# Row factors by a matmul, squares behind splits, a load table for the second phase's weights, and tiles placed elsewhere, in a hybrid decoder layer

## The chip, the cores and the metric

The kernel runs on one core of a Trainium2 chip. Its engines work side by side, each through its own queue in order: TensorE (PE) for matmuls, VectorE (DVE), ScalarE (ACT), GpSimd (POOL), and SyncE (SP), which issues most of the transfers. The metric is the device time of one execution in microseconds (us); shown is the median of three runs. A profile is one further execution taken with the hardware profiler.

## The reference

One decoder layer over 4096 new prompt tokens and 64 sample tokens (8 sequences of 8), width 1024:

```python
h = _rmsnorm(x, g_pre)
z = h @ w_in                          # (tokens, 1024) @ (1024, 2816)
cb, cc, ch, cg, q, k, v, ag, mq, mg = _split_cols(z)
conv = conv_w[0] * up[:, 0:t] + conv_w[1] * up[:, 1:t + 1] + conv_w[2] * up[:, 2:t + 2]   # up: cc * ch
out_a = jax.nn.silu(cg) * cb * conv
out_b = jax.nn.silu(ag) * o_b         # sliding-window attention of q, k, v with sinks
out_c = jax.nn.silu(mg) * o_c         # cross-attention of mq into 256 memory tokens
y = jnp.concatenate([out_a, out_b, out_c], axis=-1) @ w_out
return x + _rmsnorm(y, g_post), new_conv, new_k, new_v

def _rmsnorm(x, g):
    r = lax.rsqrt(jnp.mean(xf * xf, axis=-1, keepdims=True) + RMS_EPS)
    return (xf * r).astype(x.dtype) * g
```

The change lies in the product `h @ w_in`. Its row factors are the `r` of `_rmsnorm`: one number for each token.

## The kernel before

**The product.** The 4160 tokens are 8 blocks of 520 (`NBLK`), each two halves of 260. Tokens lie along the free dimension, channels on the 128 partitions. The 22 column tiles of `w_in` are done in three phases (`PHASES`, line 43): phase 0 takes four pairs of tiles (gates, q/k, v), phase 1 four pairs (the conv columns), phase 2 three pairs (the rest of q and mq). A pair and its index `q` is called a quad member; `q` runs over the pairs of a phase. A block of x and a pair of weights are each cut into 2 x 2 quarters, and Winograd's form of Strassen's method makes the product of them in seven steps instead of eight; `PRODUCTS` (line 40) has for each step `p` the weight operand and the x operand:

```python
PRODUCTS = (("A11", "B11"), ("A12", "B21"), ("S2", "T2"), ("S3", "T3"), ("S1", "T1"), ("S4", "B22"), ("A22", "T4"))
```

A step is written (phase, block, p). Weights that begin with S and x operands that begin with T are sums of quarters. Every operand is split in two parts that the matmul takes at full rate, hi (an ACT copy to the rounded type) and lo (a DVE subtraction); a product of one quad member is 4 x 3 matmuls (`product`, line 278: hi*hi, hi*lo, lo*hi), so a step of phases 0 and 1 is 48 matmuls of 260 columns and a step of phase 2 is 36. `w_split` (line 139) splits weights, `split` (270) and `x_split` (488) x. `evict` (286) adds the accumulators (PSUM, tags x and y in turn, two of each) into z tiles: by an ACT copy for p = 0 (line 292), by DVE otherwise (290).

**Blocks 0 and 1 of phase 0** are not done by the seven steps but by the plain eight (`PLAIN`, line 484, `plain_block`, 574), since the weights' S sums aren't there yet; here a step is written (block, s). While PE works on them, the S weights are summed (`first_sums`, 504) and split (`first_fills`), and the gate and q/k/v results are finished (`done`). What is issued beside each of the 16 plain steps stands in the table of `plain_jobs` (532); a step's jobs are dealt out behind its four products. x isn't scaled by its row factors ahead of these products: `z_rows` (525) scales z instead. From block 2 on x is scaled first (`x_gain` on ACT by the norm weight, `x_scale` on DVE by the row factors).

**The row factors.** `row_load` (203) brings 104 tokens' rows (a "nat" tile, two buffers); `row_step` (213) squares them on ACT with a running sum, five steps a block. After the fifth, POOL takes mean and power -0.5 and scatters the 520 numbers to DRAM (line 228); two row queues later SP reads them back into all 128 partitions (`rows_load`, 199: tile rb). Square j frees the buffer that load j + 2 waits for.

**Order.** In phase 0 and up to the change to phase 1, `manual_schedule` keeps each engine's instructions, DMA issues too, in the order of the program. Behind that (`in_order.close()`, line 709) a scheduler orders them by its own estimate. `flush` (119) issues the stores that were put off, at the start of the next step: by POOL's queue in phase 0, by SP's from phase 1 on (`store_queue`).

**Changes of phase.** `open_phase` (92) closes the phase's tile pools and opens those of the next in the same memory: temps (`tp`, 7, 9 and 4 buffers of 2088 bytes a partition), in phase 0 the row tiles (`natp`), and z tiles (`zp`, 5, 7 and 3). A tile of a new pool waits until what lay in its bytes is done with. Before, temps are opened first, so phase 1 has its temps over phase 0's temps, and phase 2 its z tiles over phase 1's temps. The next phase's weights are loaded in block 7: at step p + 1 those that step p used, into temps (`w_load`, 143), and split one step later (lines 728 to 739). So A11 is loaded at (0,7,1), and so on to S4, loaded at (0,7,6) and split ahead of (1,0,0), and A22 in (1,0,0).

## Time and profile before

| | us |
|---|---|
| median of three runs (lowest, highest) | 1684.39 (1681.62, 1684.4) |
| the profiled execution's own time | 1686.34 |
| its span, from first to last instruction | 1684.6 |
| granted TensorE clock, mean | 0.975 |
| DMA traffic | 306.15 MB, 182 GB/s over the span |

By stretch of the span, from counts of the matmuls of line 283: plain blocks 0 and 1 from 8.7 to 125.8 us, the rest of phase 0 to 377.5, phase 1 to 715.0, phase 2 to about 982, and attention with the output projection to the end.

The profile is read as follows. The page's first lines give each engine's busy time and share of the span; then follow 40 equal slices of the span with a digit for the busy tenths, and the clock that TensorE was granted in tenths. A timeline row has start, length, engine, line, operation, out<-in, count, and in brackets the idle time of the engine before it with what ended it. SPq and POOLq are the queues from which transfers are issued; the length there is that of the issue, not of the transfer. A row of the waits has the total, the number and the longest. A row of the chain of waits has start, length and what. In a row of windows the numbers behind the engine's busy time are counts of instructions.

### The profile page before, as it was taken

The numbers are of one execution on the slowest core, as the hardware profiler recorded it, in microseconds if no ns is written. First come the engines' busy times: TensorE is split into PE (matmuls) and PEld (weight loads), VectorE is DVE, ScalarE is ACT, GpSimd is POOL, SyncE is SP. The second block draws the span as 40 slices with busy tenths as digits, with TensorE's granted clock in tenths as the row PEclk, the third lists the DMA queues.
The fourth block names the chain that finished last, engine by engine and source line by source line (L and its number), as shares of the span: only waits on it lengthen the run. The fifth ranks groups of instructions, "written<-read, shape, count | busy, mean of one in ns | idle before, by whom it ended". The sixth has DMA issues, their size and how long they took to land.

```text
span 1684.6 us, 29573 instructions
## 1 busy us (share of the span) xinstructions
PE 1585.2 (94%) x11073; PEld 1401.4 (83%) x11073; DVE 1182.1 (70%) x2113; ACT 791.2 (47%) x2028; POOL 349.7 (21%) x590
## 2 busy tenths in 40 slices
PE   7969999998999999989999966999999999999998
PEld 7969999998999999988999953677777777777766
DVE  5548878897888778965666665766777766767743
ACT  6566556574322222533434345655555555555522
POOL 0113222211000000000000024444433344343320
PEclk9979999999999999999999977999999999999999
DMA  7778999877555333669766587767677766666152
GB/s 227 159 184 226 265 254 256 246 262 256 188 186 173 115 115 128 214 196 276 262 204 246 186 225 152 145 139 146 143 155 155 164 136 135 147 147 133 51 184 88
DMA packets 175412, 306.15 MB, mean 182 GB/s; under 512 B 31142, under 2 KB 104614, under 8 KB 175238
## 3 DMA queue, kind: packets, MB, share of 16 engines
q1 hardware_dynamic: 129061, 228.34, 43.6%
q0 software_dynamic: 46208, 75.93, 23.3%
q8 instruction: 88, 1.44, 0.3%
q14 instruction: 55, 0.44, 0.1%
HBM read 197.07 MB, written 108.12 MB: 181 GB/s over the span
## 4 chain that ended last, share of the span: by engine, by line
PE 43%; DVE 17%; ACT 7%; issue 3%; DMA 3%; POOL 3%; ACTq 0%; SPq 0%; POOLq 0%; DVEq 0%
PE c L283 30%; PE y L1213 6%; ACT sm L954 5%; DVE sm L960 3%; DVE sm L944 2%; DVE wmx L946 2%; DMA wor<-in_w_out 2%; POOL xp L909 2%; PE wt L964 1%; DVE yn L1220 1%; PE xs L901 1%; PE wo L827 1%; DVE xr L1231 1%; DVE mix L928 1%; ACT xp L905 1%
## 5 line engine op out<-in xcount | busy, mean ns | idle before, releaser
L1213 PE MATMUL y<-wo,mh 128*128 128x512 f32 (+1 forms) x1072 | 350.8, 391 | 1.4 <-DVE mh L1190 1.4
L290 DVE TENSOR_TENSOR z<-c,z 128x520 f32<-128x520 f32 (+1 forms) x308 | 194.9, 647 | 91.3 <-PE c L283 86.0
L1213 PEld LDWEIGHTS y<-wo,mh 128*128 128x128 f32 x1072 | 200.4, 188 | 42.0 <-issue 2.8
L1213 PE MATMUL y<-wo,ml 128*128 128x512 f32 (+1 forms) x520 | 202.2, 389 | 0.0
L954 ACT ACTIVATE sm<-sm,wnm 128x128 f32<-128x128 f32 x256 | 99.9, 391 | 75.7 <-DVE wnm L948 75.6
L1213 PEld LDWEIGHTS y<-wo,ml 128*128 128x128 f32 x520 | 98.1, 189 | 15.2
L941 PE MATMUL ws<-kst,q 128*128 128x256 f32 x512 | 81.8, 302 | 8.8 <-ACT sm L943 5.9
L971 POOL TENSOR_SCALAR_AFFINE_SELECT wpv<-wpt 128x512 f32<-128x512 f32 x62 | 40.0, 645 | 224.8 <-ACT wpt L966 223.9
L941 PEld LDWEIGHTS ws<-kst,q 128*128 128x128 f32 x512 | 68.3, 197 | 11.3 <-ACT sm L943 6.4
L902 DVE TENSOR_REDUCE xmx<-xs 128x2 f32<-128x512 f32 x64 | 44.2, 691 | 43.6 <-PE xs L901 43.6
L905 ACT ACTIVATE xp<-xs,xnm 128x256 f32<-128x256 f32 x128 | 59.4, 469 | 27.3 <-DVE xnm L903 27.0
L943 ACT COPY sm<-ws 128x256 f32<-128x256 f32 x128 | 44.5, 371 | 56.9 <-PE ws L941 54.0
L909 POOL TENSOR_SCALAR xp<-xp,xrd 128x256 f32<-128x256 f32 x128 | 62.9, 498 | 37.9 <-DVE xrd L906 35.1
L1221 ACT ACTIVATE y<-y 128x512 f32<-128x512 f32 (+1 forms) x66 | 38.8, 588 | 66.6 <-DVE yn L1220 66.6
L843 POOL MEMSET kst<- 128x512 f32 x1 | 0.5, 525 | 324.9 <-DVE cacc L389 324.9
L1220 DVE TENSOR_TENSOR yn<-y,gpost 128x512 f32<-128x512 f32 (+1 forms) x66 | 45.2, 684 | 30.4 <-PE y L1213 30.3
L222 ACT ACTIVATE nat<-nat 104x1024 f32<-104x1024 f32 x40 | 42.3, 1058 | 48.2 <-DMA nat<-in_x_p 48.0
L1231 DVE SCALAR_TENSOR_TENSOR xr<-yn,yst,xr 128x1024 f32<-128x1024 f32 (+2 forms) x34 | 42.5, 1253 | 29.9 <-POOL yst L1227 29.9
L964 PEld LDWEIGHTS wt<-ident,sm 128*128 128x128 f32 x256 | 28.0, 144 | 40.3 <-issue 18.1
L901 PE MATMUL xs<-mk,q 128*128 128x256 f32 x256 | 47.9, 311 | 12.3 <-ACT xp L905 8.5
L960 DVE TENSOR_TENSOR sm<-sm,wrd 128x512 f32<-128x512 f32 x64 | 54.9, 858 | 2.0
L914 PEld LDWEIGHTS xt<-ident,xp 128*128 128x128 f32 x256 | 29.7, 143 | 31.2 <-PE wo L827 12.2
(935 smaller groups left out, 5119.8 us busy)
## 6 DMA issues: line engine op xcount, KB each, us to landing
q<-qd POOLq DMA_DIRECT2D x64, 384.0 KB, 6.0
mix<-md SPq DMA_DIRECT2D x16, 1024.0 KB
xr<-in_x_p SPq DMA_DIRECT2D x32, 512.0 KB
nat<-in_x_p SPq DMA_DIRECT2D x39, 416.0 KB
o_yp<-xr SPq DMA_DIRECT2D x31, 512.0 KB
md<-th POOLq DMA_DIRECT2D x48, 260.0 KB, 7.0
qd<-zh SPq DMA_DIRECT2D x48, 260.0 KB
qd<-z SPq DMA_DIRECT2D x48, 260.0 KB
```

The lines of the kernel that those rows point to most:

```text
L283: TE.matmul(bank[:, :HW], l, r, start=first and i == 0, stop=last and i == 3 * KH - 1)
L290: add = lambda dst, other: V.tensor_tensor(dst, c, other, op=ALU.add)
L901: TE.matmul(s[:, i, :], q[:, i * P : i * P + P], third["mk"][:, part, h, :], start=part == 0, stop=part == 1)
L905: S.activation(p[:, i, :], s[:, i, :], AF.Exp, bias=nm[:, i : i + 1], scale=SCALE, accum_out=den[:, i : i + 1])
L909: G.tensor_scalar(p[:, i, :], p[:, i, :], rd[:, i : i + 1], 0.5, op0=ALU.mult, op1=ALU.mult)
L941: TE.matmul(s3[:, hh, :], self.q[:, 4 + 2 * (2 * half + hh) + kvh, i * P : i * P + P], self.kst[:, 2 * kvh + part, i * P : i * P + 2 * P], ...
L954: S.activation(sm[:, hh, :], sm[:, hh, :], AF.Exp, bias=nm[:, hh : hh + 1], scale=SCALE, accum_out=den[:, hh : hh + 1])
L960: V.tensor_tensor(sm, sm, rd.unsqueeze(2).to_broadcast([P, 4, P]), op=ALU.mult)
L964: TE.transpose(t[:, hh * P : (hh + 1) * P], sm[:, hh, :], ident)
L1213: TE.matmul(acc, self.hl[l][:, k], wo[k][:, r, c0:c1], start=j == 0, stop=j == passes * KT - 1)
L1220: V.tensor_tensor(yn[:m, c0:c1], acc[:m], gpost[:m, c0:c1], op=ALU.mult)
L1231: V.scalar_tensor_tensor(self.xr[:m, cs], yn[:m, cs], st[:m, 3:4], self.xr[:m, cs], op0=ALU.mult, op1=ALU.add)
```

## The change

Four things are changed.

1. *Block 2's row factors.* They aren't scattered to DRAM and read back. `rows_diag` makes on DVE a 104 x 520 tile of five diagonal blocks (identity times factors), `rows_product` multiplies it by a tile of ones on PE, which puts each token's factor into all 128 partitions, and ACT copies the result into the rb tile. All other blocks keep the way through DRAM.
2. *Squares behind splits.* In the table of `plain_jobs` from (0,5) on, squares (`*row`) are moved behind x splits, weight fills and finishing work; one of the twenty squares goes to step (0,2,0). The gates' copy of the sample tokens in block 0 goes from ACT to DVE.
3. *Weights at the change to phase 1* (code phase 1, the second) are loaded and split by a table, `SWITCH`, which goes ahead of a step's other jobs: A11 and S2 through the row tiles, A12 through temps, and S3, S1, S4 and A22 only in block 0 of phase 1. For the last phase the old rule stays.
4. *Places.* z tiles are opened ahead of temps in phases 1 and 2, and the row tiles ahead of temps in phase 0. So phase 1 has z over the row tiles, phase 0's temps and a little of its z, and temps over the rest of phase 0's z; phase 2 has z over phase 1's z.

```diff
+    ones = const.tile([P, P], F32, name="ones")
+    G.memset(ones, 1.0)
...
-        tp = own.enter_context(tc.tile_pool(name=f"t{ph}", bufs=(7, 9, 4)[ph]))
+
         if ph == 0:
             natp = own.enter_context(tc.tile_pool(name="nat", bufs=2))
+            tp = own.enter_context(tc.tile_pool(name="t0", bufs=7))
         zp = own.enter_context(tc.tile_pool(name=f"z{ph}", bufs=(5, 7, 3)[ph]))
+        if ph > 0:
+            tp = own.enter_context(tc.tile_pool(name=f"t{ph}", bufs=(9, 4)[ph - 1]))
...
+            if b == PLAIN_BLOCKS:
+                nat["first"] = r
+                return
             G.dma_start(rowd[b].rearrange("(i p) -> p i", p=RG), r[:RG, 0:5])
             row_spreads[b] = 2
+
+    def rows_diag():
+
+        t = nat["diag"] = temp("diag")[:RG, : 2 * HW]
+        for i in range(5):
+            V.tensor_scalar(t[:, RG * i : RG * (i + 1)], ident[:RG, :RG], nat["first"][:RG, i : i + 1], None, op0=ALU.mult)
+
+    def rows_product():
+
+        acc = pa2.tile([P, 2, 512], F32, tag="y", name="rows_y", bufs=2)[:, :, :HW]
+        for half in range(2):
+            TE.matmul(acc[:, half], ones[:RG], nat["diag"][:, HW * half : HW * half + HW], start=True, stop=True)
+        rows[PLAIN_BLOCKS] = natp.tile([P, 2 * HW], F32, tag="rb", name="rb_first")
+        S.copy(rows[PLAIN_BLOCKS].rearrange("p (a n) -> p a n", a=2), acc)
...
-            S.copy(zs[:, zsi, :], th[:, :NS])
+            V.tensor_copy(zs[:, zsi, :], th[:, :NS])
...
-            if 1 <= p < 6:
+            if 1 <= p < 6 or (b, p) == (PLAIN_BLOCKS, 0):
                 jobs.append(row_step)
...
-            (0, 5): lambda: [*sums(1, 0), *row, *sums(1, 1), *fills(1, "S2"), *row, *fills(1, "S3")],
-            (0, 6): lambda: [*parts(1, "B11"), *fills(1, "S1", "S4"), *row, *sums(3, 0)],
-            (0, 7): lambda: [*fills(3, "S2", "S3"), *row, *fills(3, "S1"), *row],
-            (1, 0): lambda: [*parts(1, "B21"), *row, *z_rows(0, 1), *row],
-            (1, 1): lambda: [*z_rows(0, 0), *done(0, 1), *row, *row],
-            (1, 2): lambda: [*row, *done(0, 0)],
-            (1, 3): lambda: [*parts(1, "B12"), *sums(2, 0), *row],
-            (1, 4): lambda: [*sums(2, 1), *fills(2, "S2"), *gains(2, "B11"), *row],
-            (1, 5): lambda: [*parts(1, "B22"), *fills(2, "S3", "S1", "S4"), *gains(2, "B21")],
-            (1, 6): lambda: [*row, *gains(2, "B12"), *scales(2, "B11", "B21"), *row],
-            (1, 7): lambda: [lambda: h_split(0), *gains(2, "B22"), *scales(2, "B12"), lambda: t_sum(0, 2, "T1"), *row,
-                             *scales(2, "B22"), *z_rows(1, 1)],
+            (0, 5): lambda: [*sums(1, 0), *sums(1, 1), *fills(1, "S2", "S3"), *row],
+            (0, 6): lambda: [*parts(1, "B11"), *fills(1, "S1", "S4"), *row, *sums(3, 0), *row],
+            (0, 7): lambda: [*fills(3, "S2", "S3", "S1"), *row],
+            (1, 0): lambda: [*parts(1, "B21"), *z_rows(0, 1), *row, *row],
+            (1, 1): lambda: [*z_rows(0, 0), *done(0, 1), *row],
+            (1, 2): lambda: [*parts(1, "B12"), *row, *done(0, 0), *row],
+            (1, 3): lambda: [*row, *sums(2, 0), *sums(2, 1), *fills(2, "S2")],
+            (1, 4): lambda: [*parts(1, "B22"), lambda: rows_diag(), *gains(2, "B11", "B21"), lambda: rows_product()],
+            (1, 5): lambda: [*row, *fills(2, "S3", "S1", "S4"), *scales(2, "B11")],
+            (1, 6): lambda: [*gains(2, "B12"), *scales(2, "B21", "B12"), *row, *row],
+            (1, 7): lambda: [lambda: h_split(0), *gains(2, "B22"), *scales(2, "B22"), lambda: t_sum(0, 2, "T1"), *row,
+                             *z_rows(1, 1)],
...
+    def next_load(nph, q, o, dst=None):
+        if dst is None:
+            raws[q, o] = w_load(nph, q, o)
+        else:
+            raws[q, o] = dst
+            DMA.dma_start(dst, w_raw(PHASES[nph][q], o) if o[0] == "A" else sd[PHASES[nph][q]][o])
...
+    last = NBLK - 1
+    SWITCH = {(0, last, 1): lambda: next_loads("A11", True),
+              (0, last, 2): lambda: next_loads("A12"),
+              (0, last, 3): lambda: next_fills("A11"),
+              (0, last, 4): lambda: [*next_fills("A12"), *next_loads("S2", True)],
+              (0, last, 6): lambda: next_fills("S2"),
+              (1, 0, 0): lambda: next_loads("S3"),
+              (1, 0, 1): lambda: [*next_loads("S1"), *next_fills("S3")],
+              (1, 0, 2): lambda: [*next_loads("S4"), *next_fills("S1")],
+              (1, 0, 3): lambda: next_loads("A22"),
+              (1, 0, 4): lambda: next_fills("S4"),
+              (1, 0, 5): lambda: next_fills("A22")}
...
-            if i > 0 and steps[i - 1][0] < 2 and steps[i - 1][1] == NBLK - 1:
+            if i > 0 and steps[i - 1][0] == 1 and steps[i - 1][1] == NBLK - 1:
...
+            if (ph, b, p) in SWITCH:
+                jobs = SWITCH[ph, b, p]() + jobs
```

`next_loads(o, True)` takes two row tiles of 1024 columns, each for two weights of 512; `next_fills(o)` splits the four.

29 lines of the change are left out of this document (19 added, 10 removed).

## Prediction

> **What bounds the kernel now.** I read the page first, for the engine that is busy nearly throughout and for the slices where it is not.
>
> ```profile
> PE 1585.2 (94%) x11073; PEld 1401.4 (83%) x11073; DVE 1182.1 (70%) x2113; ACT 791.2 (47%) x2028; POOL 349.7 (21%) x590
> ...
> PE   7969999998999999989999966999999999999998
> ...
> PEclk9979999999999999999999977999999999999999
> ```
>
> TensorE (PE) sets the time; what can be won is its idle stretches. The change touches three of them: one in slice 3 (84 to 126 us, digit 6, with its clock low) and two short ones, near 390 and 725 us, that the tenths hardly show. A step of the plain blocks and of phases 0 and 1 is 48 matmuls, one of phase 2 is 36, so the start of a step is found by counting matmuls of L283. Then I asked for windows cut at these starts. Columns: window, length, PE busy, PEld, (DVE, ACT, POOL where shown,) clock, DMA share, GB/s.
>
> ```profile
> 74.33:80.08 5.75, 5.75 (x50) 5.72 (x48) 1.00 0.60 65
> 80.08:99.94 19.86, 0.18 (x3) 0.00 (x1) 0.63 0.86 212
> 99.94:108.53 8.59, 8.59 (x48) 8.36 (x49) 0.67 0.80 137
> 108.53:114.25 5.72, 5.72 (x51) 5.72 (x49) 1.00 0.72 190
> ```
> ```profile
> 377.52:383.64 6.12, 6.02 (x50) 5.81 (x49) 6.12 (x11) 3.81 (x9) 1.74 (x4) 1.00 0.28 84
> 383.64:398.36 14.72, 7.99 (x51) 7.38 (x49) 10.44 (x13) 6.05 (x11) 4.41 (x9) 0.88 0.84 297
> 398.36:406.60 8.24, 7.71 (x48) 7.31 (x49) 5.47 (x7) 3.14 (x7) 0.84 (x2) 0.79 0.70 239
> 423.88:430.88 7.00, 6.11 (x50) 5.91 (x49) 7.00 (x8) 2.60 (x4) 0.00 (x0) 1.00 0.44 130
> 442.38:449.08 6.70, 6.03 (x51) 5.82 (x49) 6.70 (x8) 1.31 (x2) 0.00 (x0) 1.00 0.47 105
> ```
> ```profile
> 719.40:731.99 12.59, 4.76 (x38) 4.35 (x37) 5.78 (x8) 2.76 (x4) 2.92 (x5) 0.93 0.86 207
> 731.99:738.71 6.72, 6.72 (x36) 6.72 (x37) 2.95 (x6) 3.59 (x9) 0.00 (x0) 0.62 0.96 311
> 738.71:743.06 4.35, 4.35 (x39) 4.35 (x37) 2.94 (x5) 1.47 (x2) 0.00 (x0) 1.00 0.21 68
> ```
>
> A full step is 5.75 us, in phase 2 4.35. So there are three stalls. **A**, in block 1 between its fourth and fifth product: 19.86 of waiting and 8.59 - 5.75 = 2.84 in the step after it, at a clock of 0.67: 22.7. **B**, phase 0 to 1: 0.37 + 8.97 + 2.49 + 1.25 + 0.95 over 5.75 in five steps of blocks 0 and 1: 14.0. **C**, phase 1 to 2: 8.24 + 2.37: 10.6. Together 47.3 us. Next I looked at what PE waited for, and what that waited for.
>
> ```profile
> PE c L283 <- ACT hi_1B L493: 19.7, 1, 19.7
> PE c L283 <- ACT w_0A L140: 8.7, 1, 8.7
> ```
> ```profile
> PE c L283 <- ACT z L292: 6.1, 1, 6.1
> PE c L283 <- DVE lo_0B L274: 1.7, 1, 1.7
> ```
>
> **A** waits for ScalarE (ACT) to split B12 of block 1. ACT works in order, and squares of rows stand ahead of that split, each waiting for its rows from DRAM:
>
> ```profile
> 66.32 1.06 ACT L222 ACTIVATE nat<-nat 104x1024 f32<-104x1024 f32 x1 [5.45 <-DMA nat<-in_x_p]
> 71.75 1.07 ACT L222 ACTIVATE nat<-nat 104x1024 f32<-104x1024 f32 x1 [1.63 <-DMA nat<-in_x_p]
> 79.98 1.06 ACT L222 ACTIVATE nat<-nat 104x1024 f32<-104x1024 f32 x1 [0.97 <-DMA nat<-in_x_p]
> 91.55 1.06 ACT L222 ACTIVATE nat<-nat 104x1024 f32<-104x1024 f32 x1 [6.94 <-DMA nat<-in_x_p]
> 99.38 1.72 ACT L493 ACTIVATE hi_1B<-xl1B,gpre 128x260 fp32r<-128x260 f32 x4
> ```
> ```profile
> 67.84 1.20 POOL L227 TENSOR_TENSOR r<-r,mhalf 104x5 f32<-104x5 f32 x1
> 69.35 1.01 POOL L228 DMA_DIRECT2D rowd<-r  x1 [0.31 <-POOL r L227]
> 79.65 0.36 SPq L201 DMA_DIRECT2D rb<-rowd  x1
> 73.00:81.00 8.00, 7.26 (x61) 7.05 (x59) 3.22 (x5) 4.04 (x10) 2.23 (x4) 1.00 0.72 74
> 81.00:84.00 3.00, 0.00 (x0) 0.00 (x0) 0.00 (x0) 0.66 (x3) 0.00 (x0) 1.00 0.90 315
> ```
>
> Counting squares from 0, these are 9, 11, 12 and 14; 9 ends block 1's rows, 14 block 2's. After 9, POOL takes the power and scatters the 520 factors to DRAM (69.35). From 73 to 81 all queues together move 74 GB/s, then 315; SP stands at the broadcast load of these factors until 79.65. So the scatter, not the squares' arithmetic, makes the rows late.
>
> **B**: the S4 weights are loaded late and their split holds ACT, behind it the copy of PE's accumulators (L292). **C**: the same copy waits for a store, since its z tile lies where a conv temp lay.
>
> ```profile
> 380.89 0.32 SPq L147 DMA_DIRECT2D wr_0S<-sd0S  x1
> 386.01 8.10 DMA wr_3S<-sd6S
> 394.13 0.62 ACT L140 CAST w_3S<-wr_3S 128x512 fp32r<-128x512 f32 x1 [0.96 <-DMA wr_3S<-sd6S]
> ```
> ```profile
> 723.94 7.31 DMA md<-cacc
> 731.35 0.87 ACT L292 COPY z<-c 128x520 f32<-128x520 f32 x2 [4.36 <-DMA md<-cacc]
> ```
>
> **The change, part by part.** *A, squares behind splits.* Up to (0,4) nothing moves. One square less in (0,5) and (0,7) puts the load of square 8 behind block 0's broadcast, where 9's stands now: square 8 starts at 66.32, and the split of B21 behind it is where it is now. Squares 9 and 10 follow at about 69.0 and 71.75. The three copies into zs that wait for VectorE (DVE) leave ACT for DVE (three times 0.24 and their waits; DVE has room, 3.22 busy of 8 us), which hides in square 11's wait for its rows. That load is issued where 12's is now, but square 9, and so the scatter, comes 69.0 - 66.3 = 2.7 later: the slow stretch runs from 75.7 to 83.7, and 11 lands before it, near 76. Then, in the new order, comes the split of B12: 77.2, and PE wants it at 80.08. The 19.86 us are gone at this place. If 11 lands inside the slow stretch as 12 does now (79.98), 1 to 2 us stay.
>
> *A, the product with ones.* Something else is late next. The two matmuls that spread block 2's factors stand in PE's queue at the end of (1,4), and PE takes its work in order: from there it waits for square 14, the power, and the diagonal. Square 14 starts now 10.5 us after the slow stretch ends; SP has the same broadcast and the same bytes ahead of it. So 83.7 + 10.5 = 94.2; with the square and its read-out (1.15) 95.4; POOL's two operations (square's end 67.47 to 69.04) 97.0. The diagonal is five DVE instructions of 104 columns, which the trace does not show; nearest are
>
> ```profile
> L386 DVE TENSOR_SCALAR cacc<-ub,convw x16: 453/486/493, 435.8 to 718.6; 128x520 f32<-128x520 f32 x14, 128x456 f32<-128x456 f32 x2
> L386 DVE TENSOR_SCALAR cacc<-us,convw x2: 251/255/259, 436.2 to 439.8; 128x64 f32<-128x64 f32 x2
> 769.20 1.72 PE mem_acc L654 x4
> ```
>
> so 5 x 0.25 to 5 x 0.49; 104 is nearer 64, 1.3: 98.3. The matmuls are f32 like those of L654, four instructions of 512 columns in 1.72; four of 260 take 0.87: 99.2. Fifth product ends at 80.08 + 5.75 = 85.8, PE idles 12.4, and its next step is cold again, 8.59. It ends at 107.8, where now it ends at 114.25: **6.5 us won**. What this path must also pass on DVE: the sums of S weights for the third pair, which now wait for a temp until a store behind block 2's scatter lands:
>
> ```profile
> 107.28 0.69 DVE L512 TENSOR_TENSOR wa2S<-wa2A,wa2A 128x512 f32<-128x512 f32 x1 [4.46 <-DMA md<-th]
> ```
>
> Block 2's scatter is gone, so I put this temp at 90 (an estimate: its tanh follows square 12 at 80 to 82, and its store lands after the slow stretch ends at 83.7); then 0.69 and five more of 0.61 for the sums, 0.6 for S2's split and 1.7 for the low half of B22 end before 97, under square 14. Bounds of A: square 14 never late, 22.7 - 0.9 = +21.8; that temp still at 107.28, then 107.3 + 3.7 + 0.6 + 1.7 + 1.3 + 0.9 = 115.5 against 108.53: -7.0. I take the value worked out from the landing, as nothing is left of what delayed the store. Square 19 and block 3's broadcast come one step later against a PE that is 6.5 us earlier; no row prices that, it lies between 0 and one step, 5.75, and I take 0, since the factors are used two steps after the load. The memset of ones lies under PE's first wait, the 8.7 us for w_0A on ACT, and costs nothing; without that cover it would be one small POOL instruction.
>
> The Trainium skill, "TensorE: Matmul & The Clock Gate", Part 1, says that the clock falls to half after an idle window of about 3.4 us and returns after 3.4 us of work, so an estimate from that page is 1.7 us lost after each long wait. The trace agrees that the step after a wait is slow, but with 2.84 us (99.94:108.53); with 1.7 for the cold step that stays, A's gain would be 7.6 instead of 6.5.
>
> *B, loads by a table.* A11 and S2 now go through the row tiles, S3, S1, S4 and A22 (16 tiles) are loaded in phase 1 with its nine temps and split one to two steps before use. The wait of S4 for a phase-0 temp (380.89) and ACT's hold until 394.13 go. What is late next: DVE. Sixteen subtractions of 0.61 are 9.7 us in seven steps of 5.75 that hold the eviction, split and sum work already; S3 is wanted 17.25 us after phase 1 starts, and its load waits for block 7's z tiles, now under the temps. Bounds: 0 and 14.0. I leave three steps at the 1.25 that 423.88:430.88 pays with DVE full: 4 stay, **10.0 won**.
>
> *C, other places.* In phase 2 z lies over phase 1's z tiles, which DVE alone reads, last for the cacc whose store is issued at 723.94, so the copy can go then and the step at 725.9 (the 1.7 for lo_0B stays) is not held: 6.1 and the cold 2.37: **8.5 won**, bounds 0 and 10.6.
>
> **Sum.** 6.5 + 10.0 + 8.5 = 25.0. The profiled execution took 1686.3 (span 1684.6 and 1.7 around it), giving 1661.3; it is 1.9 above the median of 1684.4, so the runs should show 1659.4. All three lie on PE's own queue, and behind each PE is full for hundreds of us.
>
> **Rivals.** (1) *The whole of A goes*: square 14's load is early because the bytes ahead of it moved before the scatter. For it: block 2's B21 no longer stands behind the broadcast on SP; against: it is issued into the slow stretch. 21.8 + 18.5: 1644.1. (2) *A only turns over*: the temp is as late as now, -7.0 + 18.5: 1672.9. For it is the row at 107.28, against it that its scatter is gone. (3) *It doesn't do what it says at a phase change*: z of phase 1 now lies over phase 0's temps, and a store in flight (7.31 in the row) holds the copy there; B won 0: 1669.4. Against: POOL's stores of that block are issued early once ACT isn't held. (4) *Slower*: in phase 1 SP carries stores too, in order with the loads. If a store that waits for its producer stands ahead of S3, S1, S4 and A22, each comes a step late: 4 x 5.75 and as many cold steps, 4 x 2.84: 34.4 lost where 14.0 are lost now: -20.4 + 15.0: 1689.8. It decides when S3's last tile lands more than 17 us into phase 1; 8.10 for one load speaks against it, unless it is issued 9 us late.
>
> **Chances.** Forecast 0.50 (its own range 1651 to 1667), (1) 0.12, (2) 0.15, (3) 0.15, (4) 0.08. From 1645 to 1677 all but (4) and half of (1) are held, and a little of the rest. A run tells 0.2%, 3.4 us, from no change; only (4) ends above, and milder forms of it near the old time: faster 0.89, same 0.04, slower 0.07.
>
> **What would show it.** After: the step (1,4) starts near 80 to 82 with no wait for hi_1B; then one wait of 10 to 14 us ahead of a matmul on rows_y, released by DVE's diag; only one broadcast of rows fewer on SP; no wait on ACT z L292 near 380 and 700; the summed excess of phase 1's first two blocks at 3 to 6 us, with DVE as releaser. A is wrong if PE's wait before rows_y is under 5 or over 18 us; B if S3's load is issued later than 9 us into phase 1; C if a store still releases L292.

## The result, and the profile after

The changed kernel takes 1673.65 us in the median of seven runs (1670.3 to 1678.51), the kernel before 1684.4 beside it (seven runs, 1680.71 to 1685.72): a ratio of 0.9944, 95% interval 0.9925 to 0.9962. By the medians it is 10.75 us faster; 25.0 were forecast. Ratios, here and below, are estimated from all executions but two slow ones (6048.44 us in all_three, and 1964.64 us in the kernel before beside tsum_first) and not from the medians, whose quotient differs from them by up to 0.0009. The profiled execution took 1678.51, the slowest of the seven, with a span of 1676.8, 7.8 below the span before. So 3 of the 10.75 us stand in no trace here, and all that follows is the 7.8.

The page's first lines after the change:

```profile
PE 1585.2 (95%) x11077; PEld 1401.8 (84%) x11077; DVE 1184.1 (71%) x2124; ACT 791.1 (47%) x2023; POOL 352.5 (21%) x590
...
PE   7967999998999999999999956999999999999998
...
PEclk9989999999999999999999977999999999999999
```

PE's busy time is the same to the tenth. The 6 of slice 3 is still there, so the stall of block 1 has only become shorter; the 7 behind it, where the kernel before has a 9, is new. Steps were found as before, by counting matmuls (now line 305). Windows of the changed kernel, columns as in the prediction:

```profile
80.66:101.20 20.54, 7.41 (x54) 6.95 (x53) 11.43 (x25) 10.25 (x24) 4.09 (x7) 0.72 0.91 274
101.20:108.05 6.85, 6.85 (x51) 6.75 (x49) 4.06 (x5) 5.12 (x11) 0.47 (x1) 0.86 0.26 72
132.05:145.70 13.65, 6.30 (x49) 5.90 (x49) 6.14 (x9) 4.33 (x8) 6.04 (x11) 0.94 0.85 164
145.70:154.45 8.75, 8.06 (x48) 7.76 (x49) 7.93 (x10) 3.62 (x6) 0.00 (x0) 0.70 0.97 285
```
```profile
380.91:394.14 13.23, 6.17 (x51) 5.76 (x49) 9.76 (x13) 6.00 (x12) 3.24 (x6) 0.97 1.01 356
394.14:402.66 8.52, 8.52 (x48) 8.52 (x49) 5.95 (x9) 4.20 (x7) 0.00 (x0) 0.65 0.89 338
431.40:437.41 6.01, 5.92 (x50) 5.71 (x48) 6.01 (x16) 1.91 (x3) 0.00 (x0) 1.00 0.69 18
437.41:447.24 9.83, 7.95 (x49) 7.54 (x50) 8.76 (x11) 1.21 (x2) 0.00 (x0) 0.83 0.82 235
717.75:724.05 6.30, 4.61 (x38) 4.40 (x37) 5.17 (x7) 2.25 (x5) 0.00 (x0) 1.00 0.65 141
724.05:728.34 4.29, 4.29 (x38) 4.29 (x37) 2.37 (x3) 1.27 (x3) 0.00 (x0) 1.00 0.88 320
```

The first fence is (1,4), (1,5), and then (0,2,2) and (0,2,3), two steps of block 2 that were 7.64 and 7.01 before and are 13.65 and 8.75 now: a stall the prediction doesn't have. In the second fence (1,0,1) and (1,0,2) are nearly as long as before, (1,1,2) has become long, and (2,0,1) and (2,0,2) are short. The waits of PE, largest ones:

```profile
PE rows_y L249 <- DVE diag L243: 13.1, 1, 13.1
...
PE c L305 <- ACT hi_2T L295: 6.9, 2, 6.5
...
PE c L305 <- ACT z L314: 4.4, 1, 4.4
```

The account by stretch, each figure the difference of two step starts (after minus before): at (1,6) **-6.2** (108.05 against 114.25). Block 2 gives back 8.24, so that block 3 starts 2.0 *later* than before (171.71 against 169.67). Blocks 3 to 7 win 4.4, and phase 1 starts 2.4 earlier (375.16 against 377.52). Its first two blocks lose 0.7, block 0 of phase 2 wins **7.2**, and everything behind loses 1.0. Rounded, the sum is the -7.8.

How far one profile can be trusted is seen from the runs below, which share long stretches of code with the changed kernel. In the nine that equal it up to block 2, (1,6) starts between 106.25 and 112.04 us; in the six that equal it in blocks 0 and 1 of phase 1, these take 12.2 to 15.7 us more than full steps, and block 0 of phase 2 takes 32.4 to 33.8 (33.8 in the changed kernel, 41.0 before). The stretch behind that block takes 923.6 to 936.1 us over all versions. Of the kernel before there is one profile. So C's gain is clear; differences of three or four microseconds in the other stages are not shown by one pair of profiles.

**Block 2.** What holds hi_2T, in the timelines of POOL and of ACT:

```profile
132.52 0.99 POOL L236 DMA_DIRECT2D rowd<-r  x1 [0.30 <-POOL r L232]
133.52 1.65 POOL L132 DMA_DIRECT2D md<-th  x3
```
```profile
141.99 0.62 ACT L346 CAST zh<-z 128x520 fp32r<-128x520 f32 x1 [8.40 <-DMA md<-th]
...
144.58 1.06 ACT L295 CAST hi_2T<-xl2B 128x1040 fp32r<-128x1040 f32 x1 [0.92 <-DVE xl2B L288]
```

Block 3's scatter goes out at 132.52 and the store of a finished gate behind it at 133.52, but that store lands only at 141.96. Its temp is what the cast to zh waits for, and the split PE needs stands behind the cast on ACT. From 132 to 142 all queues moved 90 GB/s. In the kernel before, the scatter, the cast, the split and PE's first matmul on it:

```profile
129.23 1.00 POOL L228 DMA_DIRECT2D rowd<-r  x1 [0.30 <-POOL r L227]
...
141.39 0.63 ACT L324 CAST zh<-z 128x520 fp32r<-128x520 f32 x1 [2.08 <-DMA md<-th]
...
144.30 1.06 ACT L273 CAST hi_2T<-xl2B 128x1040 fp32r<-128x1040 f32 x1 [1.23 <-DVE xl2B L266]
...
145.41 0.39 PE L283 MATMUL c<-hi_2T,w_0S 128*128 128x260 f32 x1 [0.47 <-ACT hi_2T L273]
```

So the cast waited for a store behind the scatter there too, and ran within 0.6 us of its time here, although the scatter went out 3.3 us earlier. There PE came for the split near 144.9 and waited 0.47 us; here it comes near 139.2 and waits 6.45.

**Change to phase 1.** SP's issues and ACT:

```profile
382.87 0.34 SPq L152 DMA_DIRECT2D wr_0S<-sd0S  x1
...
385.83 1.65 SPq L152 DMA_DIRECT2D wr_3S<-sd6S  x1
```
```profile
389.11 0.62 ACT L145 CAST w_0S<-wr_0S 128x512 fp32r<-128x512 f32 x1 [2.82 <-DMA wr_0S<-sd0S]
...
392.98 0.62 ACT L145 CAST w_3S<-wr_3S 128x512 fp32r<-128x512 f32 x1 [1.02 <-DMA wr_3S<-sd6S]
393.50 1.08 ACT L314 COPY z<-c 128x520 f32<-128x520 f32 x2
```

The copy of PE's accumulators stands behind S3's splits, and these wait for loads issued 7.7 us into phase 1. So one late load (S3's) has taken the place of another (S4's). **Change to phase 2**, where no store holds the copy any more:

```profile
722.31 0.87 ACT L314 COPY z<-c 128x520 f32<-128x520 f32 x2 [3.30 <-DVE cacc L411]
```

### The profile page after: what moved, and what is told of

Read it like the earlier page. It is cut to its first block, busy times and chain, and to the rows that moved or that the text cites. A ratio compares the mean times of both kernels' runs of the same rounds, so it can differ in the third digit from the quotient of the medians.

```text
span 1676.8 us, 29593 instructions
## 1 busy us (share of the span) xinstructions
PE 1585.2 (95%) x11077; PEld 1401.8 (84%) x11077; DVE 1184.1 (71%) x2124; ACT 791.1 (47%) x2023; POOL 352.5 (21%) x590
## 3 DMA queue, kind: packets, MB, share of 16 engines
q1 hardware_dynamic: 128917, 228.08, 44.2%
## 4 chain that ended last, share of the span: by engine, by line
PE 55%; DVE 18%; DMA 9%; ACT 8%; issue 5%; POOL 4%; SPq 0%; ACTq 0%; POOLq 0%; DVEq 0%
PE c L305 42%; PE y L1270 6%; ACT sm L1011 5%; DMA nat<-in_x_p 3%; DVE sm L1017 3%; DVE sm L1001 2%; DMA wor<-in_w_out 2%; DVE wmx L1003 2%; POOL xp L966 2%; DVE yn L1277 1%; PE wt L1021 1%; DMA rowd<-r 1%; PE xs L958 1%; DMA md<-th 1%; DVE mix L985 1%
## 5 line engine op out<-in xcount | busy, mean ns | idle before, releaser
L1270 PEld LDWEIGHTS y<-wo,ml 128*128 128x128 f32 x520 | 98.5, 190 | 15.4
L959 DVE TENSOR_REDUCE xmx<-xs 128x2 f32<-128x512 f32 x64 | 44.2, 691 | 43.4 <-PE xs L958 43.4
L1021 PE MATMUL wt<-ident,sm 128*128 128x128 f32 x256 | 42.8, 292 | 14.0 <-DVE sm L1017 8.1
```

The lines of the kernel that those rows point to most:

```text
L1021: TE.transpose(t[:, hh * P : (hh + 1) * P], sm[:, hh, :], ident)
L1270: TE.matmul(acc, self.hl[l][:, k], wo[k][:, r, c0:c1], start=j == 0, stop=j == passes * KT - 1)
```

## The experiments

The kernels ran in groups, each on one chip with runs of the kernel before beside them, and the chips differ (that kernel's medians were 1684.05, 1682.37, 1693.6, 1682.73, 1689.75 and 1688.48). So the ratio to the kernel before on the same chip is compared: the changed kernel's is 0.9944. Where an expectation names a time, it was reckoned from 1684.4 and 1673.65, so on another chip its ratio counts. Stages are read from the profiles. "Excess" is the time of fourteen steps, blocks 0 and 1 of phase 1, over 14 x 5.75: 14.06 before, 14.73 after.

| run | median, us | before, us | ratio | 95% interval |
|---|---|---|---|---|
| rows3 | 1672.31 | 1684.05 | 0.9929 | 0.9909 to 0.9948 |
| sq19 | 1670.87 | 1684.05 | 0.9920 | 0.9901 to 0.9938 |
| place1 | 1684.67 | 1684.05 | 1.0009 | 0.9995 to 1.0023 |
| table_old | 1683.30 | 1684.05 | 0.9990 | 0.9978 to 1.0002 |
| rows1 | 1671.24 | 1682.37 | 0.9931 | 0.9907 to 0.9955 |
| dram2 | 1679.72 | 1682.37 | 0.9985 | 0.9969 to 1.0001 |
| act_order | 1680.72 | 1682.37 | 0.9981 | 0.9965 to 0.9998 |
| pool_sub | 1677.60 | 1682.37 | 0.9967 | 0.9950 to 0.9984 |
| rows3b | 1677.01 | 1693.60 | 0.9906 | 0.9887 to 0.9924 |
| places2 | 1685.24 | 1693.60 | 0.9954 | 0.9939 to 0.9968 |
| rows13 | 1669.86 | 1693.60 | **0.9862** | 0.9845 to 0.9879 |
| best1 | 1670.03 | 1693.60 | 0.9866 | 0.9848 to 0.9885 |
| less_dve | 1673.25 | 1682.73 | 0.9948 | 0.9927 to 0.9969 |
| less_dve_places2 | 1675.32 | 1682.73 | 0.9947 | 0.9928 to 0.9965 |
| tsum_first | 1683.10 | 1689.75 | 0.9966 | 0.9952 to 0.9980 |
| tsum_first_places2 | 1682.97 | 1689.75 | 0.9964 | 0.9948 to 0.9980 |
| best2 | 1669.43 | 1689.75 | 0.9876 | 0.9854 to 0.9898 |
| all_three | 1680.75 | 1688.48 | 0.9949 | 0.9930 to 0.9969 |

### A: who takes the gain back in block 2

**rows3**, block 3's factors by the product as well:

```diff
-            if b == PLAIN_BLOCKS:
+            if b in (PLAIN_BLOCKS, PLAIN_BLOCKS + 1):
...
+        if ph == 0 and b == PLAIN_BLOCKS and p == 2:
+            jobs += [rows_diag, lambda: rows_product(b + 1)]
```

> Block 3's row factors too go by the product with ones (diagonal and product in step (0,2,2)), so that no scatter of 4-byte writes falls into block 2; all else as in the changed kernel. Theory (the gain of A is given back because block 3's scatter, issued at 132.5 us, makes POOL's stores behind it land at 142 to 146 and so holds the temp of the zh cast): steps (0,2,2) and (0,2,3), 13.65 and 8.76 us now, come to under 14 us together, the 6.45 us wait for hi_2T is gone, and the time falls by 6 to 8 us to 1666 to 1668. Rival (nothing depends on the scatter; PE, 6 us earlier, simply meets the splits of block 2 before they are done): the two steps stay at 20 us or more and the time stays at 1672 to 1676.

**sq19**, square 19 where it was:

```diff
-            if 1 <= p < 6 or (b, p) == (PLAIN_BLOCKS, 0):
+            if 1 <= p < 6:
...
-            (1, 7): lambda: [..., *gains(2, "B22"), *scales(2, "B22"), ...
+            (1, 7): lambda: [..., *gains(2, "B22"), *row, *scales(2, "B22"), ...
```

> Square 19 goes back into plain step (1,7), where it was in the kernel before; all else as in the changed kernel. Theory (scatter holds the temps): the scatter goes out about 3 us earlier, at 129 to 130 us, the zh cast waits about 3 us less and step (0,2,2) shrinks from 13.65 to 10 or 11: 1670 to 1671. Rival (place of square 19 plays no part): (0,2,2) stays at 13 to 14 us, time within 1.5 us of 1673.65. A third way: the square waits on ACT in (1,7) for its rows and holds the split of block 2's first operand; then step (0,2,0) or (0,2,1) grows by what (0,2,2) loses.

ACT in rows3:

```profile
134.80 0.63 ACT L346 CAST zh<-z 128x520 fp32r<-128x520 f32 x1 [1.04 <-DMA md<-th]
...
137.73 1.06 ACT L295 CAST hi_2T<-xl2B 128x1040 fp32r<-128x1040 f32 x1 [1.25 <-DVE xl2B L288]
...
145.23 0.59 ACT L251 COPY rb_first<-rows_y 128x520 f32<-128x520 f32 x1 [5.39 <-PE rows_y L249]
```

Without the scatter the cast runs at 134.80 instead of 141.99 and the split at 137.73 instead of 144.58, so the theory's mechanism is there. But the two steps took 20.17 and the time was 1672.31, as the rival said: the new diagonal came late on DVE, and PE waited 3.76 us for it at the product. sq19 lay between: the cast ran at 139.79, (0,2,2) fell to 9.01, and block 2 took 49.3 us instead of 52.2. It began 2.2 later, but that difference is there at (1,6) already, ahead of the moved square. The third way is seen only in (0,2,1), 7.65 instead of 6.73. Block 3 starts 0.6 earlier. **rows3b** removes the flaw of rows3:

```diff
+            if (ph, b, p) == (0, PLAIN_BLOCKS, 3):
+                jobs = [rows_diag, *jobs, lambda: rows_product(PLAIN_BLOCKS + 1, "x")]
```

> Block 3's factors by the product with ones as in the run rows3, but the diagonal is made first in step (0,2,3) and the product stands at its end, one step later, so that PE need not wait for the diagonal; no scatter falls into block 2. Theory (the scatter holds the temps; in rows3 the 3.76 us wait for the diagonal ate the gain): steps (0,2,2) to (0,2,4), 28.16 us in the changed kernel, come to 19 to 21, no wait over 2 us in them, time 1665 to 1668. Rival (the gain of A is given back to anything in block 2 that is late, since PE is 6 us ahead): another wait takes the place, the three steps stay at 25 us or more and the time at 1671 or above.

Windows of its three steps:

```profile
136.05:143.04 6.99, 6.10 (x48) 5.90 (x49) 6.42 (x9) 4.71 (x8) 5.07 (x10) 1.00 0.77 263
143.04:150.40 7.36, 6.74 (x55) 6.43 (x53) 7.33 (x14) 1.69 (x4) 0.00 (x0) 1.00 1.03 320
150.40:156.30 5.90, 5.90 (x50) 5.87 (x49) 4.23 (x6) 5.67 (x11) 0.00 (x0) 1.00 0.81 201
```

20.25 us against 28.16: the stall is gone, block 2 takes 44.2 us (43.9 in the kernel before), and the ratio is 0.9906. So block 3's scatter, which goes here with its read-back, is shown to be what took A's gain back.

### A: what is left of the wait, and the product

**rows1** takes away the scatter that the prediction blamed, block 1's; **dram2** gives block 2 its scatter again under the new order of squares:

```diff
# rows1
-            if b == PLAIN_BLOCKS:
+            if b in (1, PLAIN_BLOCKS):
...
+        if b == 1:
+            late.append(lambda: G.dma_start(rowd[1].rearrange("(o n) -> o n", o=1), rows[1][0:1, :]))
...
+            (1, 2): lambda: [*parts(1, "B12"), rows_diag, *row, *done(0, 0), *row],
+            (1, 3): lambda: [*row, *sums(2, 0), *sums(2, 1), *fills(2, "S2"), lambda: rows_product(1, "x")],
# dram2
-            if b == PLAIN_BLOCKS:
-                nat["first"] = r
-                return
...
+            (1, 4): lambda: [*parts(1, "B22"), *gains(2, "B11", "B21")],
```

> Block 1's row factors too go by a product with ones (diagonal in plain step (1,2), product at the end of (1,3)); for phase 1 one row of the result is copied to DRAM, 2080 bytes in one piece. So the scatter of 520 four-byte writes at about 70 us is gone; all else as in the changed kernel. Theory (that scatter slows every queue from 73 to 82 us and so makes square 14 late): squares 13 and 14, at 89.93 and 94.04 now, come at 80 to 84 and 84 to 88, PE's wait for rows_y, 13.13 now, shrinks to 2 to 5 us, the row waits of phase 0's other blocks stay, and of the 8 to 11 us won a part is given back in block 2 behind block 3's scatter: 1663 to 1670. Rival (the rows are late because two row buffers follow each other through SP, and the bytes ahead of them, not because of the scatter): squares 13 and 14 move by less than 2 us, the wait stays over 10 us, time within 2 us of 1673.65.

> Block 2's row factors go by DRAM again, scattered after square 14 in plain step (1,3) and read back at (1,5); the order of squares and everything else as in the changed kernel. Theory (the order of the squares took away the wait for the split of B12, the product only shortens the way from square 14 to block 2's scaling): PE doesn't wait inside block 1, runs to about 104 us, and waits for block 2's scaled rows: scatter after 97, landing 10 to 12 us later, broadcast and two scales, so block 2 starts at 114 to 120 against 119.5 in the changed kernel, and its start is no more than 3 us later or earlier; time 1670 to 1677. Rival (the product is what wins A): block 2 starts at 125 us or later, as in the kernel before at 125.8, and the time goes to 1679 or above.

The same eight microseconds, in the changed kernel and in rows1 (last number GB/s):

```profile
73.00:81.00 8.00, 8.00 (x69) 8.00 (x68) 4.77 (x11) 7.20 (x16) 2.23 (x4) 1.00 0.91 102
```
```profile
73.00:81.00 8.00, 7.78 (x64) 7.61 (x64) 5.30 (x16) 6.04 (x14) 2.27 (x4) 1.00 0.98 267
```

102 against 267 GB/s, with the DMA engines 0.91 and 0.98 busy: the prediction's reading of the scatter holds, and square 14 starts at 86.19 instead of 94.04. PE no longer waits for rows_y. It waits 5.3 us for the accumulators that the new product itself holds (ACT reads them behind the squares), and block 2 starts at 114.59, 5.0 earlier. Block 3's scatter still held block 2 (a wait of 6.4 for hi_2T), and block 3 starts 4.5 earlier.

dram2 is undecided. In its trace block 2 starts at 116.89, even earlier than with the product and inside the theory's 114 to 120, but not in the theory's way: PE waits 9.0 us inside block 1, for ACT's copy of a plain step's accumulators. Block 3 starts at 171.05. Its runs, at 0.9985, fit the rival's time, and the profiled execution (1675.79) was the fastest of twelve. What the product is worth is left open.

**rows13**, both scatters gone (the edits of rows1 and rows3b together):

> The factors of blocks 1, 2 and 3 by products with ones (rows1 and rows3b together), so that no scatter is issued between 60 and 140 us; all else as in the changed kernel. Theory (the two scatters are what A's path waits for): PE's wait for rows_y is 3 to 8 us as in rows1, block 2 starts at 112 to 116 and nothing of it is given back: block 3's first step is 10 to 13 us earlier than in the changed kernel, time 1660 to 1665. Rival (what one wait sets free the next one takes): the start of block 3 is less than 6 us earlier and the time 1668 or above.

Block 3 starts at 157.89, 13.8 us earlier than in the changed kernel, as the theory said. The span is 7.5 us below the changed kernel's; the rest is lost in later stretches, by no more than these vary between profiles. Its ratio is the lowest of all runs: 0.9862, 0.82 percentage points below the changed kernel's, 1669.86 us where the kernel before takes 1693.6. The changed kernel was not run on that chip; places2 and rows3b were, and took 15.4 and 7.2 us more.

### B: why the change to phase 1 won nothing

**place1**, temps ahead of z in phase 1 again; **table_old**, the old rule of loading under the new places; **act_order**, ACT kept in program order for two steps more:

```diff
# place1
+        if ph == 1:
+            tp = own.enter_context(tc.tile_pool(name="t1", bufs=9))
         zp = own.enter_context(tc.tile_pool(name=f"z{ph}", bufs=(5, 7, 3)[ph]))
-        if ph > 0:
+        if ph == 2:
# table_old
-            if i > 0 and steps[i - 1][0] == 1 and steps[i - 1][1] == NBLK - 1:
+            if i > 0 and steps[i - 1][0] < 2 and steps[i - 1][1] == NBLK - 1:
...
-            if (ph, b, p) in SWITCH:
-                jobs = SWITCH[ph, b, p]() + jobs
# act_order
                 in_order.close()
+                if ph == 1:
+                    act_order.enter_context(tc.manual_schedule(engines={mybir.EngineType.Activation}))
...
+            if (ph, b, p) == (1, 0, 2):
+                act_order.close()
```

> Phase 1 opens temps ahead of z tiles, as in the kernel before; phase 2 keeps the new places, all else as in the changed kernel. Theory (B won nothing because S3's loads, whose temps lie over phase 0's z tiles, are issued only at 382.9 to 385.8 us, and because the copy's z tiles lie over temps whose stores are in flight): with the temps over phase 0's temps the copies on ACT wait for no store, steps (1,0,1) and (1,0,2), 13.23 and 8.52 us now, lose 5 us or more together, and the time is 1667 to 1669. Rival (the places don't matter; S3's splits stand ahead of the copy on ACT and S3 lands after 389 whatever the place): the two steps stay within 2 us of their 21.75 and the time within 1.5 us of 1673.65; if S3's temps now wait for the stores, they grow by up to 4 us.

> The weights of phase 1 are loaded and split by the old rule (step p + 1, split one step later), with the new places; all else as in the changed kernel. Theory (the loads in phase 1 are what holds ACT now, in the kernel before it was S4's load; one late load took the place of another): the excess over 5.75 of steps (1,0,0) to (1,1,2), 14.0 us in the kernel before and about 14.5 now, stays at 12 to 17 us, so the table is worth within 3 us of nothing: 1671 to 1677. Rival (the table is worth its part of B and only the places spoil it): with the old rule under the new places the stall grows to 20 us or more: 1680 or above.

> ScalarE keeps the order of the program through steps (1,0,0) and (1,0,1), so that the copies of the accumulators stand ahead of S3's four splits; the scheduler orders the rest, all else as in the changed kernel. Theory (B won nothing because the scheduler put the copies behind S3's splits, which wait for loads that land at 389 to 393): the copies run before 389, steps (1,0,1) and (1,0,2), 13.23 and 8.52 us now, come to 13 to 17 us together, S3's splits follow at 393 and cost at most 2 us at (1,0,3): 4 to 8 us won at this place, time 1666 to 1670. Rival (the copies' z tiles wait for stores in flight, whatever the order): the copies stay at 392 or later, time within 1.5 us of 1673.65.

The copy in act_order, then in place1 (with the one at the change to phase 2):

```profile
393.83 1.09 ACT L314 COPY z<-c 128x520 f32<-128x520 f32 x2 [7.99 <-DMA vd<-v]
```
```profile
389.35 1.09 ACT L316 COPY z<-c 128x520 f32<-128x520 f32 x2 [2.76 <-DMA vd<-v]
...
726.55 0.87 ACT L316 COPY z<-c 128x520 f32<-128x520 f32 x2 [0.82 <-DMA md<-cacc]
```

act_order refutes that the order on ACT is all: with S3's splits behind it, the copy waits 7.99 us for the last store of phase 0, that of the temp v, and runs at 393.83, where it ran at 393.50 behind the splits. So two holds stand one beside the other. By the order in which the pools are opened, that copy's z tile should lie over the row tiles and not over the temp v. That it waits for v's store all the same suggests that the wait belongs to the place of the whole pool, which lies over phase 0's temps; no run separates a tile's own bytes from its pool's. In place1, where the pool still covers some of those temps, the copy goes with the landing of the same store and (1,0,1) and (1,0,2) shrink from 21.75 to 15.96, as the theory asked. But block 1 then pays 3.5 more in (1,1,1) and (1,1,2). At phase 2, z lies over temps again: (2,0,1) takes 10.58 instead of 6.30, and the copy is released by a store. That undoes part of C and so confirms its cause. The runs of place1 are slowest of all by ratio (1.0009), but 4.4 of the 6.8 us by which its profile is longer lie behind block 0 of phase 2, where the code is the same. In table_old the excess is 19.60 and C stays won: above the theory's 12 to 17, just under the rival's 20, and the runs (0.9990) fit the rival. So by these profiles the table saves 4.9 us under the new places and the places cost 5.5 (19.60 against 14.06), and the two parts about cancel.

**places2** puts z where no store can hold it:

```diff
         if ph == 0:
             natp = own.enter_context(tc.tile_pool(name="nat", bufs=2))
-            tp = own.enter_context(tc.tile_pool(name="t0", bufs=7))
         zp = own.enter_context(tc.tile_pool(name=f"z{ph}", bufs=(5, 7, 3)[ph]))
+        tp = own.enter_context(tc.tile_pool(name=f"t{ph}", bufs=(7, 9, 4)[ph]))
...
-              (1, 0, 0): lambda: next_loads("S3"),
+              (1, 0, 0): lambda: next_loads("S3", "z"),
```

> Places so that phase 1's z tiles lie over the row tiles and phase 0's z tiles alone, its temps over phase 0's temps (row tiles, z, temps in this order in phase 0), and S3's raw weights go into two z tiles instead of four temps; loads, splits and all else by the table as in the changed kernel. Theory (B won nothing because phase 1's z pool lies over phase 0's temps, and its first copy therefore waits for the last stores of phase 0, landing at 389 to 391, with S3's splits ahead of it): the copies go before 388, steps (1,0,1) and (1,0,2), 21.75 us now, come to 13 to 16 us, and 6 to 8 us are won there; the wait of block 1 for DVE, 4 us, stays; time 1666 to 1669. Rival (S3's loads and splits set it, wherever z lies): the two steps stay at 19 us or more. A third way: S1's loads now wait for the stores of phase 0 and the stall moves to (1,0,4), 4 to 8 us there, time unchanged.

```profile
388.25 0.59 ACT L312 COPY z<-c 128x520 f32<-128x520 f32 x1 [1.70 <-DVE th L364]
```
```profile
386.25:396.40 10.15, 7.44 (x50) 7.24 (x49) 9.24 (x12) 4.83 (x9) 3.24 (x6) 0.83 1.00 355
396.40:402.16 5.76, 5.76 (x51) 5.76 (x49) 4.26 (x6) 2.61 (x4) 0.00 (x0) 1.00 1.01 383
430.90:439.68 8.78, 5.92 (x50) 5.71 (x49) 8.78 (x23) 1.90 (x3) 0.00 (x0) 1.00 0.78 14
439.68:449.89 10.21, 8.49 (x48) 8.29 (x49) 8.13 (x10) 1.30 (x2) 0.00 (x0) 0.67 0.83 247
```

The copy now waits for DVE, 2 us into step (1,0,1), and the two steps take 15.91, as expected (17.95 to 22.45 in the changed kernel and the six like it there). S3's loads are issued 7.7 us into phase 1 here too, but its splits stand behind the copy. Block 1 gives 3.2 us back (18.99 in the last two rows, against 15.83), and the runs show no gain (0.9954). **best1** (rows13 and places2) says the same:

> rows13 and places2 together. If the two act at places that have nothing to do with each other, the gains add up: 1653 to 1660. If a later stage is bound by transfers that start no earlier, part of it is lost: 1662 or above.

At 0.9866 it is rows13's time: places2 adds nothing. That is the rival's time; its reason, transfers that start no earlier, is not shown.

### B: block 1's stall

In (1,1,1) DVE is busy throughout (6.01 of 6.01 us, in places2 8.78 of 8.78), and behind it PE waits for the split of block 1's sum T2, which DVE makes behind 8 us of block 0's convolution. **pool_sub** gives eight subtractions to POOL; **less_dve** (and the same on top of places2) takes sixteen away, with ACT copying the raw weights in place of the low parts, so that these kernels leave out the low parts and don't compute the layer; **tsum_first** (likewise) moves the sum ahead; **all_three** puts places2, less_dve and tsum_first together:

```diff
# pool_sub, o in ("S4", "A22")
+            S.copy(w[:, 0], raw)
+            G.tensor_tensor(w[:, 1], raw, f(w[:, 0]), op=ALU.subtract)
# less_dve, o in ("S3", "S1", "S4", "A22")
+            S.copy(w[:, 0], raw)
+            S.copy(w[:, 1], raw)
# tsum_first
+            if (ph, b, p) == (1, 1, 0):
+                jobs.insert(0, lambda: t_sum(1, 1, "T2"))
```

> The low parts of S4 and A22 for phase 1, eight subtractions of 128x512, are made by POOL instead of DVE; all else as in the changed kernel. Theory (in blocks 0 and 1 of phase 1 DVE is full, so that the sums for block 1's second product come late): steps (1,1,1) and (1,1,2), 6.01 and 9.82 us now, come to 11.5 to 13.5 together; 2.5 to 4 us won, time 1669.5 to 1671.5. Rival (the sums are late for another reason, a load or ACT's order): the two stay at 15 us or more, and the time within 1.5 us of 1673.65; if POOL's subtractions hold a weight, a step from (1,0,5) to (1,0,6) grows by 2 us or more.

> The low parts of S3, S1, S4 and A22 of phase 1 (16 tiles) are not raw minus high part: ACT copies the raw weights there, so phase 1's products are wrong in their low parts, and DVE has 16 subtractions of 0.61 us, 9.8 us, less in blocks 0 and 1; all else as in the changed kernel. Theory (two bounds at the change to phase 1: the copy that waits for stores, 10.3 us of excess in (1,0,1) and (1,0,2), and DVE, which is full and pays 4.3 in (1,1,1) and (1,1,2)): the first stays at 7 to 11 us, the second goes, steps (1,1,1) and (1,1,2) at 11.5 to 12.5 us; 3 to 5 us won. Rival (the sums of block 1 are late for another reason): these two steps stay at 15 us or more.

> The same on top of places2 (the copy no longer waits for stores), so that both suspects are gone together. Theory: the excess over 5.75 of the fourteen steps of blocks 0 and 1 of phase 1, 14.7 us in the changed kernel and 11.9 in places2, falls to 3 to 6 us, and the time against places2 by 6 to 8 us. Rival (DVE isn't the bound in places2; ACT, which now gets 16 copies more, or the loads are): the excess stays at 9 us or more.

> In step (1,1,0) the sum T2 of block 1 is written ahead of block 0's finishing work (the convolution), so that DVE gets it about 8 us of DVE work earlier; nothing else is changed from the changed kernel, and the same work is done. Theory (DVE isn't short of time there, its order is: the scheduler puts T2 behind 8 us of convolution): steps (1,1,1) and (1,1,2), 15.83 us now, come to 11.5 to 12.5; 3 to 4 us won at this place. Rival (DVE is full and the convolution, put behind, holds the next step instead): the two lose less than 1.5 us, or (1,1,3) and (1,1,4) grow by what they lose.

> The same on top of places2, so that the copy's wait for stores and the late sum are both gone; the same work is done. Theory (these two are all that is left of B beside the 2.7 us wait for the low half of the first operand and its cold step): the excess over 5.75 of the fourteen steps of blocks 0 and 1 of phase 1, 11.9 us in places2, 11.4 with 16 subtractions less, falls to 4 to 6 us. Rival (DVE's load, which less_dve_places2 didn't take away wholly): it stays at 9 us or more.

> places2, the earlier sum T2 of block 1, and the 16 low parts copied by ACT instead of subtracted by DVE (so phase 1's products are wrong in their low parts), together. Theory (at the change to phase 1 three things bind in turn: the copy's wait for stores, DVE's load of 80 us in 80.5 us of PE's work, and the place of T2 behind the convolution; each alone, taken away, leaves the other two): the excess over 5.75 of the fourteen steps, 9.7 to 14.7 us in every run with one or two of them taken away, falls to 3 to 6 us. Rival (something else is the bound): it stays at 9 us or more.

The fourteen steps before, after, in less_dve and in all_three, one fence for each (third number behind the window's length: DVE):

```profile
377.52:472.08 94.56, 85.63 (x675) 83.92 (x673) 78.05 (x112) 35.79 (x59) 6.99 (x13) 0.96 0.65 211
```
```profile
375.16:470.39 95.23, 86.20 (x674) 85.06 (x673) 80.21 (x115) 38.97 (x64) 7.02 (x13) 0.95 0.71 226
```
```profile
376.23:466.89 90.66, 84.51 (x675) 83.65 (x673) 71.14 (x100) 46.79 (x80) 7.00 (x13) 0.96 0.73 237
```
```profile
379.78:472.66 92.88, 83.90 (x674) 82.45 (x673) 71.77 (x101) 46.52 (x80) 7.02 (x13) 0.98 0.76 235
```

DVE has 80.2 us of work where fourteen full steps of PE are 80.5. Taking 9.1 of it away (less_dve) brings the excess to 10.15, and (1,1,1) and (1,1,2) to 13.04: 2.8 won there, a little short of the theory. But pool_sub's excess is 10.15 too, and in its fourteen steps DVE is busy for 80.8 us, no less than the changed kernel's 80.2. So the excess does not follow DVE's busy time alone. The order alone (tsum_first) cures the two steps, 12.00, as its theory said, and then others grow:

```profile
450.94:458.26 7.32, 6.00 (x50) 5.80 (x49) 5.71 (x8) 1.06 (x1) 0.00 (x0) 1.00 0.94 328
464.02:473.94 9.92, 7.33 (x51) 7.12 (x50) 9.18 (x14) 2.23 (x3) 0.00 (x0) 0.83 0.38 138
```

(1,1,4) and (1,1,6) grow by what was won, as the rival said of (1,1,3) and (1,1,4), and the excess is 14.72 against 14.73. But (1,1,6) takes 9.77 in rows3b too, where the order is the old one, so that the reordering makes it grow is not shown. With the order on top of places2 the excess is 9.66; with less work there it is 11.38, with all three together 12.39, where the theory wanted 3 to 6. So the theory of three bounds in turn is not borne out; but since less_dve and all_three load ACT with what they take from DVE, no run shows the fourteen steps with less work on both. In all_three, 2.97 is left in the first three steps, 2.9 in (1,0,3) and (1,0,4), where DVE's low halves follow late high halves from ACT (which has the sixteen copies, 46.5 us of work instead of 39), 2.2 in (1,1,2) and 3.9 in (1,1,6). What sets the last 9 to 12 us at this place **stays open**. Shown is that the two steps of the copy fall to 15.9 us, below all kernels with the changed kernel's code there, that with less work on DVE or another order the stall in block 1 is smaller, and that no single change brings the excess below 10.15, where unchanged code has 12.2 to 15.7.

pool_sub is its own lesson, told at the end. **best2** put rows13, places2 and the earlier sum together:

> rows13, places2 and the earlier sum T2 together. If the three gains add up: 0.5 points of ratio below rows13 (0.9862), so 0.980 to 0.984. If a later stage takes it back: 0.986 or above.

0.9876, no better than rows13: the rival.

## Why the prediction was right or wrong

**A, right at its place, then lost.** (1,4) starts at 80.66, the wait for rows_y is 13.1 (predicted 12.4, bounds 5 to 18) with DVE's diagonal as releaser, and at (1,6) 6.2 us are won where 6.5 were forecast. That it came so near is luck: the nine other profiles of the same code give 2.2 to 8.0. A part of the sum was off: the cold step (1,5) took 6.85, not 8.59, and the f32 product 1.6 instead of 0.87 since it ran cold itself; together 1.9 us of cold, where 2.84 was taken from before. That is near the estimate of 1.7 that the prediction worked out from the Trainium skill, "TensorE: Matmul & The Clock Gate", Part 1; but step (1,0,2) after a wait of 4.4 lost 2.77 (8.52 at a clock of 0.65), so both sizes occur. The lower bound of A, -7.0, leaves out the cold step that the forecast counts; with it the bound is -9.8, and rival (2)'s time 1675.7.

**The step that failed first** is the sentence behind the sum, "behind each PE is full for hundreds of us", with "Square 19 and block 3's broadcast come one step later ... I take 0". In the kernel before, the cast to zh already stood until a store behind block 3's scatter landed, and the split behind it came 0.47 us late for PE. In the changed kernel cast and split ran at nearly the same time (141.99 and 144.58), and PE, there earlier, waited 6.45 us: A's gain uncovered a wait that was there. The prediction had this chain in block 1 (the row at 107.28, "until a store behind block 2's scatter lands") and did not follow POOL's queue to the stores behind block 3's scatter, to the temps they hold, to ACT's cast, to the split. Block 2 took 52.2 us instead of 43.9, a price of 8.24; without the scatter (rows3b) it took 44.2. The later square is the smaller part: with it back (sq19), block 2 took 2.8 less and block 3 started 0.6 earlier, inside the bound of 5.75 that I had set. Blocks 3 to 7 then won 4.4, which I cannot put down to the change: kernels with the same code and places show an excess of 1.6 to 6.2 us in that stretch (before: 6.6).

**B, the second step that failed**, +10.0 forecast, -0.7 found. The sentence that failed is "The wait of S4 for a phase-0 temp (380.89) and ACT's hold until 394.13 go", with "What is late next: DVE". S4's wait went, but ACT's hold stayed: the copy stood behind S3's splits until 393.50. act_order shows a second hold beside it, until 393.83, the store in flight of rival (3), whose price for B (0) was right and to which I gave 0.15. My reason against that rival, "POOL's stores of that block are issued early", was beside the point: they are issued from 381.9 on, among S3's loads, and in act_order the copy waits for the last of them to land. S3's load came 7.7 us into phase 1, inside my bound of 9, so that sign did not tell. The second half of B's estimate, "4 stay" for a full DVE, was met in size by (1,1,1) and (1,1,2) with 4.3, but by luck: whatever is won ahead of it is partly paid there (7.5 in places2), and what sets it is open.

**C, right**, 7.2 of 8.5, and clear of the spread. No store releases the copy, DVE does. The rest is a new wait for a low half in (2,0,4), 5.57 instead of 4.31. place1 undid part of it by its cause.

**The sum.** 6.5 + 10.0 + 8.5 = 25.0 became 6.2 + 0 + 7.2, less 8.2 in block 2, plus 4.4 in blocks 3 to 7, less 1.7 (0.7 at B, 1.0 behind): 7.8 in the profile, 10.75 in the runs. Rival (1) did not occur; even in rows1, with block 1's scatter gone, block 2 starts 11.2 us earlier than in the kernel before, and not 21.8. Rival (2), with A lost, has by its own time (1672.9) come nearest to the runs, but for another reason. Rival (4) did not occur: S3's last tile landed near 393, 17.8 us into phase 1 and so just past its point of 17, but SP was not held by a store ahead of it, and the loads behind it were not late for PE.

## What to carry to other kernels

Follow a moved transfer into its queue: ask which stores stand behind it, which buffers they hold, and which engine waits for those, also two blocks on. When a wait is taken away, the next one can already be there, covered by the first (0.47 us of it showed before, 6.45 after); look for engines that stand waiting now while PE does not care. Where one region is reused across phases, lay the tile needed first over memory that only engines read: that won 7.2 us at phase 2, while a store in flight held the copy at phase 1. Count the work of the next engine over the whole stretch (80.2 us of DVE beside 80.5 of PE) before counting a wait as won, and take several profiles of the same code before reading a few microseconds in a stage.
